# A decoder layer's w_down stage: the fourth weight sum and three operand sets split ahead of time, two weight chunks split early, and the last norms on VectorE

## The chip, the cores and the metric

The kernel runs on one core of a Trainium2 chip. The metric is device microseconds of one execution; a result is the median over several runs.

## What is computed

One post-norm decoder layer on x of 512 tokens by 1024 features, all float32:

```
p = x @ w_in                      -> u_A, v_A, q, k, v, gate_A, gate_B
y_A = GELU(u_A) * (tril(W_s) @ LN(GELU(v_A)) + b)      per chunk of 128 tokens
y_B = causal block attention over q, k, v              8 heads of 64, rotary
x = LN(alpha*x + (sig(gate_A)*(y_A @ w_a) + sig(gate_B)*(y_B @ w_b)) @ w_out)
[a | g] = causal depthwise conv3(x @ w_up)             w_up: 1024 x 5632
x = LN(alpha*x + (GELU(a)*g) @ w_down)                 w_down: 2816 x 1024
```

## The kernel before

Every float32 product is made of three fast matmuls. A tile is split into a high part, rounded by a ScalarE copy (L91), and a low part, the rest, by a VectorE subtraction (L92); `mm3` (L169) multiplies high by high, high by low and low by high. So each weight chunk (128 x 1024, half a megabyte) has to be loaded, split on two engines, and only then is multiplied. `issue` (L134) loads chunks into four raw tiles; `split_to` (L149) splits them in order, into a ring of three `wh`/`wl` pairs or, for chunks in `resident` (L115), into units of the pool `big`. After the split of chunk i it issues the load of chunk i + 4, which waits until its raw tile has been split. `chunk(i)` (L165) splits up to chunk i + 2 and hands over chunk i. The instructions of an engine run in the order in which the code issues them, and loads and stores stand in the queue of the engine that issues them, here SP.

The last two stages matter here. **w_up** (L645 to L675) takes 22 iterations n of two chunks, 48 matmuls of 128x128 by 512 columns per iteration. After the first chunk of iteration n comes `conv_ffn_tail(n - 1)` (L587): two ScalarE Identity instructions, four VectorE taps (L595), a GELU (L597), a product; for odd n - 1 also three sums and the split of the result into `fu[p]`, the left operands of w_down (p = 0 to 10). Its tiles, `cv` and `sa`, come from the pool `t4` of four buffers. **w_down** is computed with a Strassen-like scheme of seven products: it needs four plain blocks of the weights (B11, B12, B21, B22) and four sums of them (Tq, T3, T2, T4). The sums are made during w_up: `stage_load` (L628) fetches a megabyte of the four blocks for one p, `stage_add` (L632) makes four sums on VectorE, and `stage_store` (L639) writes them to `sums` in DRAM, from where they are loaded later as ordinary chunks. The stages stand at iterations 2, 3, 5, 7, ... 21.

`FIRST` (L699) is the first pass over six groups g of p (two p each, the last one) with B11, Tq, T3 and T2, 264 matmuls. Meanwhile `second_operands` (L685) makes from `fz` and `fu` the operands `fv[p]` of the second pass: two 256-column sums, two splits. `SECOND` (L743) covers groups 0 to 2 of B21, T4 and B22, then `rest` (L757) covers groups 3 to 5, one output tile of 128 tokens after the other: T4 for tokens 0 and 1, then B21 and B22 for tokens 2 and 3. `after_first` (L730) combines the first pass's results into the residual `x01b`/`x23b`. `finish` (L766) is a LayerNorm of one token tile, `norm` (L525), and its store; with `quick` false the second half of the norm is a ScalarE scaling (L539) and a GpSimd addition (L540), with `quick` true one VectorE instruction per half (L537). The last token tile's norm is written out at L791 to L803.

The pool `big` has 18 units of 8 KB per partition; a tile that finds none free waits for the last reader of an older one, a store among them.

Of the kernel before, what the change touches and what calls it, by code (L numbers as in the profile page):

```python
# [18 lines left out]
P = 128  # L19
# [34 lines left out]
TAIL = 3  # L54
FIRST = [(w, g) for g in range(len(GROUPS))
         for w in (("B11", "Tq", "T3", "T2") if g < len(GROUPS) - 1 else ("T2", "B11", "T3", "Tq"))]
SECOND = [(w, g) for g in range(TAIL) for w in ("B21", "T4", "B22")]
LAST = [(w, g) for w in ("T4", "B21", "B22") for g in range(TAIL, len(GROUPS))]
DOWN = FIRST + SECOND + LAST
C_SECOND = C_DOWN + len(FIRST)  # L60
C_LAST = C_SECOND + len(SECOND)
N_CHUNKS = C_DOWN + len(DOWN)
PLAIN = {"B11": 0, "B12": 1, "B22": 2, "B21": 3}
SUMS = {"Tq": 0, "T3": 1, "T2": 2, "T4": 3}
# [3 lines left out]
def decoder_layer(ctx: ExitStack, tc: tile.TileContext, wts, wd, xT, x, rope, wsp, par, sgu_gb, ln_gb, out):  # L68
# [18 lines left out]
    def f32(ap):  # L87
        return ap.bitcast(F32)
# [26 lines left out]
    resident = set(range(C_OUT + 4, C_OUT + 8)) | {C_UP + 3} | set(range(C_LAST, N_CHUNKS))  # L115
# [7 lines left out]
    sums = dram.tile([4, P, NQ * 512], F32, name="sums")  # L123
# [461 lines left out]
    fu, fz, held = {}, [], {}  # L585

    def conv_ffn_tail(n, ps):  # L587
        p, second = n // 2, n % 2
        ac = t4.tile([P, 2, 512], F32, tag="t4", name=f"cv{n}")
        fs = [s * NP + p + second * NQ for s in range(2)]  # L590
        for s, f in enumerate(fs):
            nc.scalar.activation(ac[:, s], ps[s], AF.Identity, bias=cb[:, f:f + 1], scale=cw[:, 2, f:f + 1])  # L592
        for s, f in enumerate(fs):
            for tap, sh in ((1, 1), (0, 2)):
                nc.vector.scalar_tensor_tensor(ac[:, s, sh:], ps[s][:, :S - sh], cw[:, tap, f:f + 1], ac[:, s, sh:],  # L595
                                               op0=ALU.mult, op1=ALU.add)
        nc.scalar.activation(ac[:, 0], ac[:, 0], AF.Gelu)  # L597
        if not second:

            held[p] = t4.tile([P, 4, 256], F32, tag="t4", name=f"sa{p}")  # L600
            nc.vector.tensor_mul(held[p][:, 2:4].rearrange("p a b -> p (a b)"), ac[:, 0], ac[:, 1])
            return
        if p % 4 == 0:
            fz.append(unit([P, 4, 2, 256], F32, f"fz{p // 4}"))
        z, sa = fz[p // 4][:, p % 4], held.pop(p)
        nc.vector.tensor_mul(z.rearrange("p a b -> p (a b)"), ac[:, 0], ac[:, 1])
        nc.vector.tensor_sub(sa[:, 0], z[:, 0], sa[:, 2])
        nc.vector.tensor_add(sa[:, 1], sa[:, 3], sa[:, 0])
        nc.vector.tensor_sub(sa[:, 2], sa[:, 3], sa[:, 2])
        fu[p] = unit([P, 2, 4, 256], F32R, f"fu{p}")  # L610
        split(fu[p][:, 0], fu[p][:, 1], sa)
# [13 lines left out]
    stage_at = {n: p for p, n in enumerate([2] + list(range(3, NP, 2)))}  # L625
# [12 lines left out]

    def stage_store(p):  # L639
        nc.sync.dma_start(sums[:, :, cols(p)].rearrange("a p c -> p a c"), stage.pop(p))  # L640
# [16 lines left out]
    for n in range(2, NP):  # L657
        ps = up_banks(n)
        for s in range(2):
            up_part(ps[s], *chunk(C_UP + 2 * n + s), 0, S)  # L660
            if s == 0:
                if n - 1 in stage_at:
                    stage_store(stage_at[n - 1])
                if n == 3:
                    for i in range(2):
                        nc.sync.dma_start(x1s[i], xres[i].rearrange("p a d -> p (a d)"))
                if n + 1 in stage_at:
                    stage_load(stage_at[n + 1])
                conv_ffn_tail(n - 1, prev)
                if n in stage_at:  # L670
                    stage_add(stage_at[n])
        prev = ps
    stage_store(NQ - 1)
    split_to(C_DOWN + 2)
    conv_ffn_tail(NP - 1, prev)  # L675


    lnp = unit([P, 2, D], F32, "lnp2")
    xres = unit([P, 2, D], F32, "x01b"), unit([P, 2, D], F32, "x23b")
# [3 lines left out]
    fv = {}  # L683
# [14 lines left out]

    for n, (w, g) in enumerate(FIRST):  # L699
        hl = chunk(C_DOWN + n)  # L700
        p0, np_ = GROUPS[g]
        for kk in range(np_):
            for i in range(2):
                prod(acc[w][i], hl, kk, fu[p0 + kk], left[w], i, p0 + kk == 0, p0 + kk == NQ - 1)
        if n == 2:
            for i in range(2):
                nc.sync.dma_start(xres[i].rearrange("p a d -> p (a d)"), x1s[i])
        if n == 6:
            nc.sync.dma_start(lnp.rearrange("p a d -> p (a d)"), ln_gb[1].partition_broadcast(P))
        if g > 0 and n % 4 in (1, 3) and g < len(GROUPS) - 1:  # L710
            second_operands(p0 - 2 + n % 4 // 2)
# [31 lines left out]
    for n, (w, g) in enumerate(SECOND):  # L743
        hl = chunk(C_SECOND + n)
# [5 lines left out]
        if n in (1, 3):  # L750
            after_first(n // 2)
        if n in (4, 6, 8):
            second_operands(NQ - 3 + (4, 6, 8).index(n))
# [3 lines left out]
    def rest(w, ps, i, start, lo=0, hi=512):  # L757
        for g in range(TAIL, len(GROUPS)):
            if (w, g) not in res:
                res[w, g] = chunk(C_LAST + LAST.index((w, g)))  # L760
# [5 lines left out]
    def finish(t):  # L766
        norm(t, sts[t], 1, False)
        nc.sync.dma_start(out[t * P:(t + 1) * P, :], xt(t))
# [108 lines left out]
```

## Time and profile before

| | us |
|---|---|
| median of 3 runs | 711.59 (711.11 to 713.39) |
| the profiled execution | 711.34 |
| its span, first to last instruction | 709.6 |
| TensorE busy | 689.1 (97%) |
| weight loads on TensorE | 568.0 (80%) |
| VectorE busy | 475.6 (67%) |
| ScalarE busy | 313.0 (44%) |
| GpSimd busy | 48.0 (7%) |

The profiled execution is 0.25 us under the median, and 1.74 us of it lie outside the span. Busy shares are means over stages with different limits; the rows further down show single stretches. PE is TensorE, DVE VectorE, ACT ScalarE, POOL GpSimd, SP the queue that issues most DMAs. A row of a timeline gives start, duration, engine, line, instruction, output, inputs and shape; in brackets stands the idle time before it and what ended it. Matmuls overlap: one of 512 columns lasts 0.39 us, and the next can begin 0.23 us after it.

### The profile page before, as it was taken

The numbers are of one execution on the slowest core, as the hardware profiler recorded it, in microseconds if no ns is written. First come the engines' busy times: TensorE is split into PE (matmuls) and PEld (weight loads), VectorE is DVE, ScalarE is ACT, GpSimd is POOL, SyncE is SP. The second block draws the span as 40 slices with busy tenths as digits, with TensorE's granted clock in tenths as the row PEclk, the third lists the DMA queues.
The fourth block names the chain that finished last, engine by engine and source line by source line (L and its number), as shares of the span: only waits on it lengthen the run. The fifth ranks groups of instructions, "written<-read, shape, count | busy, mean of one in ns | idle before, by whom it ended". The sixth has DMA issues, their size and how long they took to land.

```text
span 709.6 us, 8593 instructions
## 1 busy us (share of the span) xinstructions
PE 689.1 (97%) x3293; PEld 568.0 (80%) x3293; DVE 475.6 (67%) x721; ACT 313.0 (44%) x466; POOL 48.0 (7%) x44
## 2 busy tenths in 40 slices
PE   8999999999999999999999999999999989999875
PEld 7887888888888888888988888888888867887744
DVE  6576755454455267656588778777787695778985
ACT  5184552545445454513253444434434343556430
POOL 0213000000001000043100000000000000000042
PEclk9999999999999999999999999999999998999977
DMA  9513131222124422450159556654557548756531
GB/s 345 194 60 119 60 119 65 83 63 88 60 62 171 154 90 94 142 179 1 38 201 333 193 201 221 216 197 149 179 208 236 179 148 296 242 149 203 175 136 61
DMA packets 34841, 108.41 MB, mean 153 GB/s; under 512 B 2928, under 2 KB 3056, under 8 KB 33776
## 3 DMA queue, kind: packets, MB, share of 16 engines
q1 hardware_dynamic: 33936, 103.93, 43.1%
q0 software_dynamic: 432, 3.15, 1.1%
q10 hardware_dynamic: 432, 0.79, 0.3%
q8 instruction: 26, 0.43, 0.3%
q14 instruction: 15, 0.12, 0.1%
HBM read 92.12 MB, written 15.73 MB: 152 GB/s over the span
## 4 chain that ended last, share of the span: by engine, by line
PE 84%; DVE 8%; ACT 2%; issue 2%; DMA 2%; POOL 1%; DVEq 0%; SPq 0%; ACTq 0%; POOLq 0%
PE up L175 10%; PE up L176 10%; PE up L177 10%; PE g L175 5%; PE g L176 4%; PE g L177 4%; PE c L172 3%; PE c L173 3%; PE c L171 3%; DVE wl L92 2%; PE Y L364 2%; PE o L173 2%; PE o L171 2%; PE o L172 2%; PE tp L349 1%
## 5 line engine op out<-in xcount | busy, mean ns | idle before, releaser
L92 DVE TENSOR_TENSOR wl<-raw,wh 128x1024 fp32r<-128x1024 f32 (+1 forms) x120 | 144.0, 1206 | 135.6 <-ACT wh L91 135.2
L91 ACT ACTIVATE wh<-raw 128x1024 fp32r<-128x1024 f32 (+1 forms) x123 | 127.6, 1042 | 136.9 <-PE up L176 67.0
L175 PE MATMUL up<-x1T,wh 128*128 128x512 f32 (+1 forms) x368 | 139.3, 378 | 0.0
L177 PE MATMUL up<-x1T,wl 128*128 128x512 f32 (+1 forms) x368 | 138.1, 375 | 0.0
L176 PE MATMUL up<-x1T,wh 128*128 128x512 f32 (+1 forms) x368 | 138.1, 375 | 0.0
L176 PEld LDWEIGHTS up<-x1T,wh 128*128 128x128 f32 x368 | 69.3, 188 | 12.6
L177 PEld LDWEIGHTS up<-x1T,wl 128*128 128x128 f32 x368 | 69.2, 188 | 12.5
L175 PEld LDWEIGHTS up<-x1T,wh 128*128 128x128 f32 x368 | 69.2, 188 | 12.4
L595 DVE SCALAR_TENSOR_TENSOR cv<-up,prm,cv 128x511 f32<-128x511 f32 x88 | 63.8, 746 | 1.5
L175 PE MATMUL g<-xT,wh 128*128 128x512 f32 x128 | 52.1, 407 | 0.0
L176 PE MATMUL g<-xT,wh 128*128 128x512 f32 x128 | 50.1, 392 | 0.0
L177 PE MATMUL g<-xT,wl 128*128 128x512 f32 x128 | 50.0, 390 | 0.0
L171 PE MATMUL c<-wh,fu 128*128 128x512 f32 x88 | 35.3, 401 | 2.2 <-ACT wh L91 2.2
L172 PE MATMUL c<-wl,fu 128*128 128x512 f32 x88 | 35.6, 405 | 0.9 <-DVE wl L92 0.9
L173 PE MATMUL c<-wh,fu 128*128 128x512 f32 x88 | 35.3, 401 | 0.0
L592 ACT ACTIVATE cv<-up,prm 128x512 f32<-128x512 f32 x44 | 31.5, 764 | 3.2 <-PE up L177 3.2
L330 ACT ACTIVATE p<-s,nm 128x128 f32<-128x128 f32 (+3 forms) x32 | 16.9, 527 | 33.4 <-DVE nm L329 32.2
L530 POOL TENSOR_TENSOR rs<-rs,mhalf 128x1 f32<-128x1 f32 x7 | 6.8, 973 | 360.8 <-DVE rs L529 360.8
L175 PEld LDWEIGHTS g<-xT,wh 128*128 128x128 f32 x128 | 24.0, 188 | 7.1 <-issue 2.7
L177 PEld LDWEIGHTS g<-xT,wl 128*128 128x128 f32 x128 | 24.0, 188 | 5.4
L597 ACT ACTIVATE cv<-cv 128x512 f32<-128x512 f32 x22 | 13.9, 633 | 32.5 <-DVE cv L595 32.4
L176 PEld LDWEIGHTS g<-xT,wh 128*128 128x128 f32 x128 | 24.1, 188 | 4.1
(226 smaller groups left out, 1287.7 us busy)
## 6 DMA issues: line engine op xcount, KB each, us to landing
raw<-wts SPq DMA_DIRECT2D x95, 512.0 KB, 3.3
st<-wd SPq DMA_DIRECT2D x11, 1024.0 KB, 8.5
sums<-st SPq DMA_DIRECT2D x11, 1024.0 KB, 6.5
raw<-sums SPq DMA_DIRECT2D x20, 512.0 KB, 4.3
raw<-wd SPq DMA_DIRECT2D x15, 512.0 KB, 4.4
x<-x POOLq DMA_DIRECT2D x2, 1024.0 KB, 6.3
x1s<-x SPq DMA_DIRECT2D x2, 1024.0 KB, 10.9
xr<-xT SPq DMA_DIRECT2D x3, 512.0 KB, 7.4
```

The costliest lines, as they stand in the source:

```text
L91: nc.scalar.activation(hi, src, AF.Copy)
L92: sub.tensor_sub(lo, src, f32(hi))
L171: nc.tensor.matmul(ps, ah, wh, start=start, stop=False)
L172: nc.tensor.matmul(ps, ah, wl, start=False, stop=False)
L173: nc.tensor.matmul(ps, al, wh, start=False, stop=stop)
L175: nc.tensor.matmul(ps, wh, ah, start=start, stop=False)
L176: nc.tensor.matmul(ps, wh, al, start=False, stop=False)
L177: nc.tensor.matmul(ps, wl, ah, start=False, stop=stop)
L330: nc.scalar.activation(pr[:, s, :N], sc[s][:, :N], AF.Exp, bias=nm[:, s:s + 1], accum_out=sm[:, s:s + 1])
L364: nc.tensor.matmul(Y[hp][s * 64:s * 64 + 64, t * P:(t + 1) * P], v[:, k, (2 * hp + s) * 64:(2 * hp + s) * 64 + 64], tr[:, s, k * P:(k + 1) ...
L592: nc.scalar.activation(ac[:, s], ps[s], AF.Identity, bias=cb[:, f:f + 1], scale=cw[:, 2, f:f + 1])
L595: nc.vector.scalar_tensor_tensor(ac[:, s, sh:], ps[s][:, :S - sh], cw[:, tap, f:f + 1], ac[:, s, sh:], op0=ALU.mult, op1=ALU.add)
```

## The change

The fourth sum T4 is no longer stored as a sum and split in the second pass: `stage_split` splits it in w_up, one iteration after its stage, into a `th` tile of the pool `t4`, and `stage_store`, a further iteration later, writes three sums to `sums` and the split pair to `sum4`. The second pass loads pairs (`load_t4`) straight into units. For p = 8, 9, 10 the operands `fv` are made in the conv tail, stored to `fvs` and loaded back (`load_fv`); the other eight `second_operands` begin one group earlier. The stages now stand at iterations 2, 3, 4, 5, 7, ... 19. The last combination, p = 10, becomes `combine_last`, called in the second step of the first pass. B21 and B22 of group 0 are split in the first pass, into units. `ready` says how many of the last six chunks are split at each step of SECOND, and `after_first` moves from steps 1 and 3 to steps 0 and 1. `finish` calls `norm` with `quick` true. The reloads of x and of the norm's weights move to later steps.

```diff
@@ -52,16 +52,19 @@
 TAIL = 3
+NZ = 8
 FIRST = [(w, g) for g in range(len(GROUPS))
          for w in (("B11", "Tq", "T3", "T2") if g < len(GROUPS) - 1 else ("T2", "B11", "T3", "Tq"))]
-SECOND = [(w, g) for g in range(TAIL) for w in ("B21", "T4", "B22")]
-LAST = [(w, g) for w in ("T4", "B21", "B22") for g in range(TAIL, len(GROUPS))]
-DOWN = FIRST + SECOND + LAST
-C_SECOND = C_DOWN + len(FIRST)
-C_LAST = C_SECOND + len(SECOND)
+EARLY = {12: ("B21", 0), 16: ("B22", 0)}
+LAST = [(w, g) for w in ("B21", "B22") for g in range(TAIL, len(GROUPS))]
+DOWN = []
+for _n, _key in enumerate(FIRST):
+    DOWN += [EARLY[_n], _key] if _n in EARLY else [_key]
+DOWN += [(w, g) for g in range(1, TAIL) for w in ("B21", "B22")] + LAST
+AT = {key: C_DOWN + i for i, key in enumerate(DOWN)}
 N_CHUNKS = C_DOWN + len(DOWN)
 PLAIN = {"B11": 0, "B12": 1, "B22": 2, "B21": 3}
-SUMS = {"Tq": 0, "T3": 1, "T2": 2, "T4": 3}
+SUMS = {"Tq": 0, "T3": 1, "T2": 2}
@@ -112,7 +115,7 @@
     state = {"dma": 0, "split": 0}
-    resident = set(range(C_OUT + 4, C_OUT + 8)) | {C_UP + 3} | set(range(C_LAST, N_CHUNKS))
+    resident = set(range(C_OUT + 4, C_OUT + 8)) | {C_UP + 3} | {AT[key] for key in LAST + list(EARLY.values())}
     with_chunk = {
@@ -120,7 +123,9 @@
-    sums = dram.tile([4, P, NQ * 512], F32, name="sums")
+    sums = dram.tile([3, P, NQ * 512], F32, name="sums")
+    sum4 = dram.tile([2, P, NQ * 512], F32, name="sum4")
+    fvs = dram.tile([NQ - NZ, P, 6 * 256], F32, name="fvs")
     x1s = dram.tile([2, P, 2 * D], F32, name="x1s")
@@ -582,7 +587,7 @@
-    fu, fz, held = {}, [], {}
+    fu, fz, fv, held = {}, [], {}, {}
@@ -600,15 +605,32 @@
             return
-        if p % 4 == 0:
-            fz.append(unit([P, 4, 2, 256], F32, f"fz{p // 4}"))
-        z, sa = fz[p // 4][:, p % 4], held.pop(p)
-        nc.vector.tensor_mul(z.rearrange("p a b -> p (a b)"), ac[:, 0], ac[:, 1])
-        nc.vector.tensor_sub(sa[:, 0], z[:, 0], sa[:, 2])
-        nc.vector.tensor_add(sa[:, 1], sa[:, 3], sa[:, 0])
-        nc.vector.tensor_sub(sa[:, 2], sa[:, 3], sa[:, 2])
-        fu[p] = unit([P, 2, 4, 256], F32R, f"fu{p}")
-        split(fu[p][:, 0], fu[p][:, 1], sa)
+        if p < NZ:
+            if p % 4 == 0:
+                fz.append(unit([P, 4, 2, 256], F32, f"fz{p // 4}"))
+            z = fz[p // 4][:, p % 4]
+        else:
+            z = ac[:, 1].rearrange("p (a b) -> p a b", a=2)
+
+        def combine():
+            sa = held.pop(p)
+            nc.vector.tensor_mul(z.rearrange("p a b -> p (a b)"), ac[:, 0], ac[:, 1])
+            nc.vector.tensor_sub(sa[:, 0], z[:, 0], sa[:, 2])
+            nc.vector.tensor_add(sa[:, 1], sa[:, 3], sa[:, 0])
+            nc.vector.tensor_sub(sa[:, 2], sa[:, 3], sa[:, 2])
+            fu[p] = unit([P, 2, 4, 256], F32R, f"fu{p}")
+            split(fu[p][:, 0], fu[p][:, 1], sa)
+            if p >= NZ:
+                s4 = ac[:, 0, 0:256]
+                nc.vector.tensor_sub(s4, sa[:, 1], z[:, 1])
+                v2 = unit([P, 2, 3, 256], F32R, f"fvp{p}")
+                split(v2[:, 0, 0:2], v2[:, 1, 0:2], z)
+                split(v2[:, 0, 2], v2[:, 1, 2], s4)
+                nc.sync.dma_start(fvs[p - NZ], f32(v2.rearrange("p a b c -> p (a b c)")))
+
+        if p == NQ - 1:
+            return combine
+        combine()
@@ -622,7 +644,8 @@
     stage = {}
-    stage_at = {n: p for p, n in enumerate([2] + list(range(3, NP, 2)))}
+    stage_at = {n: p for p, n in enumerate([2, 4] + list(range(3, 20, 2)))}
+    stage_at = dict(zip(sorted(stage_at), range(NQ)))
     cols = lambda p: slice(p * 512, (p + 1) * 512)
@@ -636,8 +659,15 @@
+    def stage_split(p):
+        th = t4.tile([P, 2, 512], F32R, tag="t4", name=f"th{p}")
+        split(th[:, 0], th[:, 1], stage[p][:, 3])
+        stage[p] = stage[p], th
+
     def stage_store(p):
-        nc.sync.dma_start(sums[:, :, cols(p)].rearrange("a p c -> p a c"), stage.pop(p))
+        s, th = stage.pop(p)
+        nc.sync.dma_start(sums[:, :, cols(p)].rearrange("a p c -> p a c"), s[:, 0:3])
+        nc.sync.dma_start(sum4[:, :, cols(p)].rearrange("a p c -> p a c"), f32(th))
@@ -659,28 +689,26 @@
             if s == 0:
-                if n - 1 in stage_at:
-                    stage_store(stage_at[n - 1])
+                if n - 2 in stage_at:
+                    stage_store(stage_at[n - 2])
                 if n == 3:
...
                 conv_ffn_tail(n - 1, prev)
+                if n - 1 in stage_at:
+                    stage_split(stage_at[n - 1])
                 if n in stage_at:
...
         prev = ps
-    stage_store(NQ - 1)
-    split_to(C_DOWN + 2)
-    conv_ffn_tail(NP - 1, prev)
-
-
-    lnp = unit([P, 2, D], F32, "lnp2")
-    xres = unit([P, 2, D], F32, "x01b"), unit([P, 2, D], F32, "x23b")
+    split_to(C_DOWN + 3)
+    combine_last = conv_ffn_tail(NP - 1, prev)
+
+
     acc = {"B11": banks_of("c1", (0, 1)), "Tq": banks_of("c5", (2, 3)), "T3": banks_of("c7", (4, 5)),
...
     left = {"Tq": 0, "T2": 1, "T3": 2, "B11": 3}
-    fv = {}
@@ -696,19 +724,46 @@
+    ring_order = [key for key in FIRST + [(w, g) for g in range(TAIL) for w in ("B21", "B22")]
+                  if AT[key] not in resident]
+
+    def take(key):
+
+        split_to(AT[key] + 1)
+        n = ring_order.index(key)
+        for nxt in ring_order[n + 1:n + 3]:
+            split_to(AT[nxt] + 1)
+        return whl.pop(AT[key])
+
+    t4w = {}
+
+    def load_t4(g):
+        p0, np_ = GROUPS[g]
+        t4w[g] = unit([P, 2, CH], F32R, f"t4w{g}")
+        nc.sync.dma_start(f32(t4w[g][:, :, :np_ * 512]), sum4[:, :, p0 * 512:(p0 + np_) * 512].rearrange("a p c -> p a c"))
+
+    def load_fv(p):
+        fv[p] = unit([P, 2, 3, 256], F32R, f"fv{p}")
+        nc.sync.dma_start(f32(fv[p].rearrange("p a b c -> p (a b c)")), fvs[p - NZ])
+
     for n, (w, g) in enumerate(FIRST):
-        hl = chunk(C_DOWN + n)
+        hl = take((w, g))
+        if n == 1:
+            combine_last()
         p0, np_ = GROUPS[g]
...
                 prod(acc[w][i], hl, kk, fu[p0 + kk], left[w], i, p0 + kk == 0, p0 + kk == NQ - 1)
-        if n == 2:
-            for i in range(2):
-                nc.sync.dma_start(xres[i].rearrange("p a d -> p (a d)"), x1s[i])
-        if n == 6:
-            nc.sync.dma_start(lnp.rearrange("p a d -> p (a d)"), ln_gb[1].partition_broadcast(P))
-        if g > 0 and n % 4 in (1, 3) and g < len(GROUPS) - 1:
-            second_operands(p0 - 2 + n % 4 // 2)
+        if n % 2 and 3 <= n < 3 + 2 * NZ:
+            second_operands((n - 3) // 2)
+        if n == 15:
+            load_t4(0)
+            xres = [None, unit([P, 2, D], F32, "x23b")]
+            nc.sync.dma_start(xres[1].rearrange("p a d -> p (a d)"), x1s[1])
+        if n == 19:
+            xres[0] = unit([P, 2, D], F32, "x01b")
+            nc.sync.dma_start(xres[0].rearrange("p a d -> p (a d)"), x1s[0])
+            load_t4(1)
@@ -740,31 +795,49 @@
     right = {"T4": 0, "B21": 1, "B22": 2}
-    for n, (w, g) in enumerate(SECOND):
-        hl = chunk(C_SECOND + n)
+    ready = {0: 0, 1: 0, 2: 0, 3: 0, 4: 1, 5: 3, 6: 4, 7: 6, 8: 6}
+    for n, (w, g) in enumerate((w, g) for g in range(TAIL) for w in ("B21", "T4", "B22")):
+        if w == "T4":
+            hl = t4w[g]
+            hl = hl[:, 0], hl[:, 1]
+        elif g == 0:
+            hl = whl.pop(AT[w, g])
+        else:
+            hl = take((w, g))
+        if ready[n]:
+            split_to(AT[LAST[ready[n] - 1]] + 1)
         p0, np_ = GROUPS[g]
...
                      w == "B22" and i == 1 and p0 + kk == 2 * TAIL - 1)
-        if n in (1, 3):
-            after_first(n // 2)
-        if n in (4, 6, 8):
-            second_operands(NQ - 3 + (4, 6, 8).index(n))
+        if n in (0, 1):
+            after_first(n)
+        if n == 2:
+            load_t4(2)
+            load_fv(NZ)
+            load_fv(NZ + 1)
+        if n == 4:
+            load_fv(NZ + 2)
+        if n == 5:
+            for i in range(TAIL, len(GROUPS)):
+                load_t4(i)
+            lnp = unit([P, 2, D], F32, "lnp2")
+            nc.sync.dma_start(lnp.rearrange("p a d -> p (a d)"), ln_gb[1].partition_broadcast(P))
     nc.vector.tensor_sub(xt(3)[:, cB], xt(3)[:, cB], onto["B22"][1])
...
             if (w, g) not in res:
-                res[w, g] = chunk(C_LAST + LAST.index((w, g)))
+                res[w, g] = (t4w[g][:, 0], t4w[g][:, 1]) if w == "T4" else whl.pop(AT[w, g])
             p0, np_ = GROUPS[g]
...
     def finish(t):
-        norm(t, sts[t], 1, False)
+        norm(t, sts[t], 1, True)
         nc.sync.dma_start(out[t * P:(t + 1) * P, :], xt(t))
```

## Rows read from the trace of the kernel before

**Rows 1.** Windows: us, busy of each engine (instructions), granted clock, DMA share, GB/s.

```profile
378.00:389.00 11.00, 11.00 (x50) 9.13 (x49) 9.41 (x14) 3.67 (x5) 0.00 (x0) 1.00 1.02 409
...
576.90:592.30 15.40, 12.24 (x41) 9.31 (x41) 10.15 (x13) 6.31 (x7) 0.00 (x0) 0.78 0.63 197
...
592.30:643.70 51.40, 51.14 (x226) 41.98 (x224) 36.23 (x53) 26.80 (x39) 0.00 (x0) 1.00 0.71 233
...
643.70:681.40 37.70, 35.26 (x150) 27.76 (x150) 35.98 (x56) 17.84 (x25) 1.55 (x2) 1.00 0.56 181
...
681.40:695.00 13.60, 8.51 (x21) 5.71 (x20) 8.83 (x12) 4.27 (x6) 5.79 (x5) 0.62 0.19 77
```

**Rows 2.** Timeline of TensorE at the start of the first pass.

```profile
576.94 0.39 PE L171 MATMUL c<-wh,fu 128*128 128x512 f32 x1
...
582.15 0.39 PE L173 MATMUL c<-wh,fu 128*128 128x512 f32 x1
...
584.75 0.50 PE L171 MATMUL c<-wh,fu 128*128 128x512 f32 x1 [2.21 <-ACT wh L91]
...
586.20 0.80 PE L172 MATMUL c<-wl,fu 128*128 128x512 f32 x1 [0.95 <-DVE wl L92]
...
592.23 0.39 PE L171 MATMUL c<-wh,fu 128*128 128x512 f32 x1
```

**Rows 3.** Timeline of ScalarE and VectorE in w_up and at its end.

```profile
390.60 1.22 DVE L92 TENSOR_TENSOR wl<-raw,wh 128x1024 fp32r<-128x1024 f32 x1
...
565.54 1.06 ACT L91 ACTIVATE fu<-sa 128x1024 fp32r<-128x1024 f32 x1 [5.89 <-DMA sums<-st]
...
577.64 2.97 DVE L595 SCALAR_TENSOR_TENSOR cv<-up,prm,cv 128x511 f32<-128x511 f32 x4
...
583.78 1.22 DVE L92 TENSOR_TENSOR fu<-sa,fu 128x1024 fp32r<-128x1024 f32 x1 [1.12 <-ACT fu L91]
...
584.92 3.49 DVE L92 TENSOR_TENSOR wl<-raw,wh 128x1024 fp32r<-128x1024 f32 x3
```

**Rows 4.** Timeline of TensorE in the second pass.

```profile
643.71 0.50 PE L171 MATMUL c<-wh,fv 128*128 128x512 f32 x1 [0.28 <-ACT keptT L719]
...
681.26 0.39 PE L173 MATMUL c<-res,fv 128*128 128x512 f32 x1
...
686.17 0.80 PE L171 MATMUL c<-res,fv 128*128 128x512 f32 x1 [4.53 <-ACT res L91]
...
694.71 0.39 PE L173 MATMUL c<-res,fv 128*128 128x512 f32 x1
...
701.85 0.28 PE L173 MATMUL c<-res,fv 128*128 128x256 f32 x1
```

**Rows 5.** Groups by line and form, 352 us to the end: count, busy, mean.

```profile
L92 DVE TENSOR_TENSOR wl<-raw,wh 128x1024 fp32r<-128x1024 f32 x69 | 83.6, 1222 | 50.9 <-ACT wh L91 50.7
...
L92 DVE TENSOR_TENSOR fv<-fz,fv 128x512 fp32r<-128x512 f32 x11 | 7.5, 685 | 0.0
```

**Rows 6.** Timeline of VectorE in the second pass and the tail.

```profile
645.66 1.28 DVE L520 SCALAR_TENSOR_TENSOR x23b<-x23b,c 128x512 f32<-128x512 f32 x2
...
649.35 0.69 DVE L520 SCALAR_TENSOR_TENSOR x23b<-x23b,keptT 128x512 f32<-128x512 f32 x1
...
653.57 0.75 DVE L523 BATCH_NORM_STATS2 st<-x01b 128x6 f32<-128x256 f32 x2
...
676.92 0.68 DVE L773 TENSOR_TENSOR x01b<-x01b,c 128x512 f32<-128x512 f32 x1
...
678.79 1.40 DVE L533 SCALAR_TENSOR_TENSOR x01b<-x01b,mv,lnp 128x512 f32<-128x512 f32 x2
...
702.16 0.42 DVE L785 TENSOR_TENSOR x23b<-x23b,c 128x256 f32<-128x256 f32 x1 [0.91 <-PE c L173]
```

**Rows 7.** DMA issues: size of each, median us from issue to landing.

```profile
x23b<-x1s SPq DMA_DIRECT2D x1, 1024.0 KB, 10.7
...
raw<-sums SPq DMA_DIRECT2D x4, 256.0 KB, 2.7
```

## The prediction

> **What bounds the kernel now.** First the windows: TensorE has no idle time where w_up runs at the granted clock 1.00, and it loses time in two places only [rows 1]. Between 576.9 and 592.3 us it is busy for 12.24 of 15.40 us at a mean clock of 0.78; between 681.4 and 695.0 us for 8.51 of 13.60 us at 0.62. From 643.7 to 681.4 us VectorE is busy for 35.98 of 37.70 us: the second pass is bound by VectorE, which splits weights, prepares operands and combines there, while the first pass (36.23 of 51.40 us) is not.
>
> Then the timeline of TensorE, for the price of each place. Its pace is (582.15 - 576.94)/23 = 0.2265 us per 512-column matmul [rows 2]. At the start of the first pass the 25th matmul was due at 582.38; full pace is back at 592.23, 15 matmuls later, which need 3.40 us: 6.45 us are lost. The third chunk's `wl` came 3.59 us late (second matmul due 582.61, begun 586.20), and then the matmuls ran at half pace, the lower level of the clock (1.2 GHz), for another 2.86. What was late is read from the other engines [rows 3]: ScalarE stood 5.89 us behind a `fu` tile whose memory a stage store still held, and VectorE came to the third chunk's `wl` only after the last conv tail, at 584.92.
>
> In the second pass, 183 matmuls of 512 columns and 30 of 256 (0.12 each) need 45.1 us from 643.71; the last ends at 701.97, so 13.2 us are lost [rows 4], most of them behind 681.26, where a weight split sat on ScalarE behind the norms and the clock then fell.
>
> **The change part by part.**
>
> *Work moved into w_up.* Each of 11 stages gains one 512-column split, 0.69 us of VectorE by the `fv` form [rows 5], and three operand pairs gain a sum and two splits, 0.42 + 0.69 + 0.42 = 1.53 us each: 7.5 + 4.6 = 12.1 us of VectorE. Cover: chunks are split two ahead, and an iteration like that of 378 to 389 us leaves VectorE free for 1.6 of 11 us [rows 1]. The tightest spot is iteration 5, as stages now sit at 2, 3, 4 and 5: its second chunk's `wl` ended at 391.8 [rows 3] and was due 16.5 iterations of 48 matmuls before 576.94, at 397.5. Ahead of it come two splits and the four sums of a new stage, 2 x 0.69 + 2.77 = 4.2 us: it ends at 396.0, 1.5 us early, and the next iteration has no combination. I take nothing; if the lead is less than this, up to 2 us of wait, once.
>
> *DMAs in w_up.* A stage writes 1.25 MB in two stores in place of 1 MB, three more stores write operands. The heaviest iteration, the third (x1s out, 2 MB), ran at 409 GB/s [rows 1]; it now loads a stage, but stores none. Taken as nothing: two splits and four raw tiles lie between a load and its use.
>
> *End of w_up.* The last stage moves from iteration 21 to 19, and one `fz` unit goes, so the 5.89 us wait goes. What is late next: `split_to(C_DOWN + 3)` puts the third chunk ahead of the tail. It waits for the ring buffer of the last w_up chunk, free at about 577.1; `wh` 1.06, `wl` until 579.4, in time for 582.4. The four taps (2.97 [rows 3]) end at 582.4, the fourth chunk's `wl` at 584.0, due at 585.3. But `combine_last` is issued ahead of the fifth chunk's split on ScalarE and VectorE. From the last tap (580.61) to the end of the `fu` split (585.00) this work took 4.4 us before [rows 3]; now it ends at 588.4, the pair for p = 10 follows, ScalarE reaches the fifth `wh` at about 589.1, and `wl` ends at 591.4. It is due as second matmul at 588.05: 3.35 us late against 3.59 before. So the wait moves by two chunks and shrinks by 0.25 us. Its clock cost lies between nothing and the 2.86 us of before. The nearest row is that of before, where waits of 2.21 and 0.95 us took the clock down [rows 2]; the new ones, about 2.1 and 1.1, are their like, so I take 2.86: gain 0.25 us.
>
> The Trainium skill ("TensorE: Matmul & The Clock Gate", Part 1) says that the array's recent activity sets its clock and that the moment of judgement isn't tied to the kernel's start. By this rule nearly the same idle time may fall either way; the row alone says it falls.
>
> *First pass.* Two chunk splits (1.22 each), `combine_last` and earlier `second_operands` go onto a VectorE that had 15 of 51 us free [rows 1]: nothing. The loads of t4w0, x23b, x01b and t4w1 (4 MB) stand among raw loads on SP's queue; four raw tiles cover them.
>
> *Second pass.* Out of VectorE go 5.5 chunk splits of T4 (6.7 us), those of B21 and B22 of group 0 (2.4) and three `second_operands` (3 x 1.95, the pair's 1.53 and another sum), 15 us where it was 95% busy. So all 13.2 us of TensorE's loss could go. Two things come back.
>
> First, SP. All loads stand in one queue, and a raw load waits until its buffer has been split. VectorE is free of the copies at 646.94, spends 2 x 4.97 us (649.35 to 654.32, [rows 6]) on `after_first`, now back to back, and splits B21(2), B22(2), B21(3), B21(4) until 658.1, 659.3, 660.5 and 661.7. The raw load of the last chunk waits for that, and the loads of t4w3, t4w4, t4w5 and `lnp2` stand behind it, at 662 to 663.5. Ahead of them on the DMA engines are 2.25 MB of raw tiles and fv10. At 409 GB/s (2.56 us per MB) with some 2 us until landing (256 KB took 2.7, of which 0.64 is transfer [rows 7]) they land at about 669.4, 671.9, 673.2 and 675.8. TensorE wants t4w3 at 643.71 + 108 x 0.2265 = 668.2: a wait of 1.2; six matmuls later t4w4: 1.1; t4w5 and `lnp2` are in time. Cost 2.3 us. Bounds: nothing, if they land as alone; 4 us, if they land as late as the 10.7 us of x23b [rows 7].
>
> Second, the norms. `finish` leaves ScalarE and GpSimd, and VectorE takes 1.40 us more for each of three. A norm with its sum and stats is then 1.87 (676.92 to 678.79) + 2 x 1.35 = 4.6 us [rows 6]. Tokens end 3.4 us apart on TensorE, so VectorE runs full from the first T4 end on: 4.6 + 4.6 + 1.4 + 4.6 + 1.4 + 0.9 = 17.5 us to the last L785, against 17.1 us of TensorE's. Cost 0.4 us, bounds 0 and 1. From L785 at 702.16 to the end nothing changes.
>
> **Sum.** Second pass -13.2 + 2.3 + 0.4 = -10.5; start of the first pass -0.25. The span of 709.6 us becomes 698.8; 711.34 - 709.6 = 1.74 lie around it, and the profiled run stands 0.25 under the median of 711.59. So 711.59 - 10.75 = **700.8 us**.
>
> **Rivals.**
>
> *A, the clock holds* at the fifth chunk: 2.86 less, 697.9. For it: the new idle time is a little shorter. Against it: the waits before [rows 2].
>
> *B, the T4 loads come in time*: 2.3 less, 698.5; with A 695.6. For it: the windows show the queue far from full in the second pass (0.56 [rows 1]). Against it: it is empty because SP waits.
>
> *C, the clock also falls at the T4 waits*, or the loads come later: 2.9 more, 703.7; with the wait of 2 in iteration 5, 705.7. Against it: the smaller waits before 681 us left the clock at 1.00 [rows 1].
>
> *D, slower*: the new `th` tiles share four buffers with the conv tails and are held until both stores have landed. If a store took longer than about 20 us (the next `th` in the same buffer), ScalarE would stand there with the weight splits behind it. One such wait is 5.89 us [rows 3]; less a lead of some 3 us, 11 stages cost 32 us: about 733. Against it: one megabyte took 10.7 us behind 2.5 others [rows 7].
>
> *E, nothing moves*: the second pass gives its waits back as waits for loads: 711. Against it: 15 us leave the engine that bounds it.
>
> **Chances.** Forecast 0.42, A 0.23, B with or without A 0.14, C 0.15, D 0.04, E 0.02. All but D and E are faster by over 0.3% (2.1 us, about what a measurement of this kernel can tell from no change): faster 0.94, same 0.02, slower 0.04. The range goes from B with A, 695.5, to C with its wait, 705.5.
>
> **What would show it.** Right: TensorE's wait for `wl` at the start of the first pass stands at the fifth chunk, with 3 to 3.5 us; no wait for `res` on ScalarE; TensorE waiting about 2 us for a DMA into t4w3 or t4w4; VectorE without a gap from the first `finish` to the end; no PE wait in w_up. Wrong: a PE wait inside w_up, a wait of ScalarE for a store, or the second pass with the clock below 1.00 before its last matmuls.

## The result and the profile after

The changed kernel takes 699.66 us (699.61 to 702.1, 4 runs) against 711.46 (711.11 to 713.39, 4 runs): a ratio of 0.9837 [0.981, 0.9865]. The forecast was 700.8 us, from 695.5 to 705.5. The profiled execution took 702.1 us, 2.4 more than the median, with a span of 700.1; it stands against the 709.6 of before.

First the waits of TensorE in the changed kernel (engine, tile, line, what it waited for: us in total, times, longest):

```profile
PE c L176 <- DMA t4w<-sum: 2.3, 1, 2.3
PE c L176 <- ACT wh L94: 1.7, 1, 1.7
PE c L176 <- ACT keptT L774: 1.6, 1, 1.6
...
PE c L177 <- DVE wl L95: 0.8, 1, 0.8
```

The two left out belong to the start of the kernel, and a last one of 0.2 us lies ahead of w_up. All others are in three places: the start of the first pass, its end, and T4 in the second pass. The windows, with columns as in [rows 1]:

```profile
378.00:389.00 11.00, 11.00 (x50) 9.12 (x49) 10.29 (x15) 3.36 (x5) 0.00 (x0) 1.00 1.02 398
577.20:595.40 18.20, 15.76 (x61) 12.32 (x61) 14.51 (x21) 9.75 (x13) 0.00 (x0) 0.91 0.50 173
595.40:643.50 48.10, 46.50 (x206) 38.13 (x205) 34.80 (x50) 26.67 (x37) 0.00 (x0) 1.00 0.78 262
643.50:667.90 24.40, 24.40 (x108) 20.17 (x108) 20.19 (x28) 9.13 (x12) 0.00 (x0) 1.00 0.85 321
667.90:674.00 6.10, 3.83 (x11) 2.62 (x10) 1.29 (x2) 0.63 (x1) 0.00 (x0) 0.72 1.04 418
674.00:692.00 18.00, 18.00 (x93) 15.39 (x92) 15.90 (x33) 0.00 (x0) 2.77 (x3) 1.00 0.26 103
```

In w_up (378 to 389) VectorE went from 9.41 to 10.29 us of 11 and TensorE has no gap, as before [rows 1]. In the second pass up to T4 VectorE is busy for 20.19 of 24.40 us, where it was 35.98 of 37.70 [rows 1], and TensorE runs there without a gap for 24.4 us. The timeline of TensorE gives the sum:

```profile
577.24 0.39 PE L176 MATMUL c<-wh,fu 128*128 128x512 f32 x1
...
589.97 0.50 PE L176 MATMUL c<-wh,fu 128*128 128x512 f32 x1 [1.69 <-ACT wh L94]
591.23 0.50 PE L177 MATMUL c<-wl,fu 128*128 128x512 f32 x1 [0.76 <-DVE wl L95]
...
591.80 0.62 PE L176 MATMUL c<-wh,fu 128*128 128x512 f32 x1
...
595.44 0.39 PE L176 MATMUL c<-wh,fu 128*128 128x512 f32 x1
...
643.47 0.50 PE L176 MATMUL c<-res,fv 128*128 128x512 f32 x1 [1.60 <-ACT keptT L774]
...
667.86 0.39 PE L178 MATMUL c<-wh,fv 128*128 128x512 f32 x1
670.52 0.80 PE L176 MATMUL c<-t4w,fv 128*128 128x512 f32 x1 [2.27 <-DMA t4w<-sum]
...
673.25 0.61 PE L176 MATMUL c<-t4w,fv 128*128 128x512 f32 x1
...
673.93 0.39 PE L178 MATMUL c<-t4w,fv 128*128 128x512 f32 x1
...
692.59 0.28 PE L178 MATMUL c<-res,fv 128*128 128x256 f32 x1
```

From the second pass's first matmul to the last it took 58.14 us before (643.71 to 701.85 [rows 4]) and takes 49.12 now: -9.02. The first pass went from 66.77 to 66.23: at its start 4.60 us are lost where 6.45 were, at its end 1.3 more than before. It starts 0.30 later, and the end behind the last matmul is 0.24 shorter. Together -9.5 us, the difference of the spans.

What was late is in the timelines of the other two engines (against [rows 3]); first VectorE at the start of the first pass:

```profile
579.45 2.97 DVE L600 SCALAR_TENSOR_TENSOR cv<-up,prm,cv 128x511 f32<-128x511 f32 x4
...
583.83 0.69 DVE L617 TENSOR_TENSOR cv<-cv 128x512 f32<-128x512 f32 x1
...
586.90 1.23 DVE L95 TENSOR_TENSOR fu<-sa,fu 128x1024 fp32r<-128x1024 f32 x1 [1.13 <-ACT fu L94]
...
589.95 2.36 DVE L95 TENSOR_TENSOR wl<-raw,wh 128x1024 fp32r<-128x1024 f32 x2 [0.52 <-ACT wh L94]
```

The combination (583.83 to 589.4) stands between the taps and the fifth chunk's `wl`; the wait of 5.89 us for a store [rows 3] is gone. And ScalarE at the first pass's end:

```profile
641.88 1.06 ACT L94 ACTIVATE wh<-raw 128x1024 fp32r<-128x1024 f32 x1 [1.62 <-PE c L178]
642.84 2.04 ACT L774 ACTIVATE keptT<-c 128x512 f32<-128x512 f32 x4
```

The copies `keptT`, for which TensorE waits until 643.47, stand behind the split of B22(1) (B22 of group 1). For the idle time ahead of that split the profile names a matmul, but the last one that read this ring buffer's older chunk began at 640.12 and lasts 0.39 us. The chunk's load was issued at 635.18 us and took 6.6 us to land, so the split waited for its raw tile. In e8 below, the trace names the load itself:

```profile
639.33 1.06 ACT L94 ACTIVATE wh<-raw 128x1024 fp32r<-128x1024 f32 x1 [2.05 <-DMA raw<-wd]
```

### The profile page after: what moved, and what is told of

It is laid out like the page before. It is cut to its first block, busy times and chain, and to the rows that moved or that the text cites. A ratio compares the mean times of both kernels' runs of the same rounds, so it can differ in the third digit from the quotient of the medians.

```text
span 700.1 us, 8629 instructions
## 1 busy us (share of the span) xinstructions
PE 684.1 (98%) x3293; PEld 566.2 (81%) x3293; DVE 476.6 (68%) x729; ACT 309.4 (44%) x465; POOL 40.0 (6%) x38
## 4 chain that ended last, share of the span: by engine, by line
PE 87%; DVE 8%; DMA 2%; ACT 1%; issue 1%; POOL 0%; DVEq 0%; SPq 0%; ACTq 0%
PE up L181 11%; PE up L180 11%; PE up L182 11%; PE g L180 5%; PE g L181 4%; PE g L182 4%; PE c L176 3%; PE c L177 3%; PE c L178 3%; PE Y L369 2%; PE o L177 2%; PE o L178 2%; PE o L176 2%; DMA t4w<-sum 1%; PE tp L354 1%; DVE st L528 1%
## 5 line engine op out<-in xcount | busy, mean ns | idle before, releaser
L95 DVE TENSOR_TENSOR wl<-raw,wh 128x1024 fp32r<-128x1024 f32 (+1 forms) x115 | 137.8, 1206 | 123.5 <-ACT wh L94 123.1
L94 ACT ACTIVATE wh<-raw 128x1024 fp32r<-128x1024 f32 (+1 forms) x118 | 122.4, 1040 | 128.1 <-PE up L181 61.5
```

The source lines that it names most:

```text
L94: nc.scalar.activation(hi, src, AF.Copy)
L95: sub.tensor_sub(lo, src, f32(hi))
```

## The experiments

All of them were timed in turn with the kernel before, whose median on the chips used was 709.6 to 710.7 us; the ratio is to that, and the range in brackets is its 95% interval.

**The changed kernel once more (e1).**

> The changed kernel as it is, timed beside the others. Its profiled run took 702.1 us, three runs without a profile 699.6 to 699.7. If the clock falls in some executions and holds in others at the two waits of TensorE (fifth chunk, t4w3; together 1.7 + 2.2 us at half clock in the profiled run), single times should lie at 699.6 or some 2 us above, nothing between; if the profile itself costs 2.4 us, only the profiled run lies at 702.

701.25 us (698.92 to 702.72, 5 runs), ratio 0.9864 [0.9847, 0.988]. Neither alternative held: the times are 698.92, 700.47, 701.25, 701.5 and 702.72 us, and the profiled one is the second fastest. Their mean granted clock goes with them in the main: 0.996 at 698.92 and 700.47, 0.990 at 702.72. The window from the first pass's start to 600 us shows one place of it, in four kernels that are the same up to there. The changed kernel's window:

```profile
577.20:600.00 22.80, 20.36 (x81) 16.08 (x81) 17.79 (x26) 12.50 (x17) 0.00 (x0) 0.93 0.54 177
```

The same in this run (e1):

```profile
577.40:600.00 22.60, 20.16 (x88) 16.15 (x87) 18.40 (x27) 12.89 (x18) 0.00 (x0) 1.00 0.55 184
```

In e3, below:

```profile
577.80:600.00 22.20, 19.76 (x73) 15.51 (x72) 16.78 (x25) 11.34 (x15) 0.00 (x0) 0.85 0.52 169
```

In e4, below:

```profile
577.00:600.00 23.00, 20.56 (x89) 16.44 (x89) 18.76 (x27) 13.20 (x18) 0.00 (x0) 1.00 0.57 188
```

All four have the same two waits, 1.7 and 0.76 us, in the same place. The clock held in two and fell to the half level in two, for different lengths. Against the pace of 0.2265 us per matmul, 4.6, 3.0, 5.9 and 3.1 us are lost by 600 us; the chunk is 2.9 us late in all four, so the clock's share is 1.7, about nothing, 3.0 and about nothing.

**The last combination later (e2).** The combination p = 10 goes from step 1 of the first pass to step 2, behind the fifth chunk's split; its operand pair to step 18.

```diff
-        if n == 1:
+        if n == 2:
             combine_last()
+        if n == 18:
+            pair_last()
```

> The last combination is called at step 2 of the first pass, after the split of the fifth chunk was issued, and the operand pair of p = 10 at step 18. Theory 1 (the order on ScalarE and VectorE makes the wait at the fifth chunk): the waits of 1.69 and 0.76 us vanish or shrink below 0.5, the clock stays up there, and the time falls by the 2.9 us of the wait, by up to 4.6 with its clock: 695 to 697 us. Rival (the fifth chunk's weights land late): the wait stays, 699.7.

697.81 us (697.58 to 698.62, 5 runs), 0.982 [0.9807, 0.9833], 3.4 us under e1 on the same chip, and 0.8 above the forecast. TensorE's only waits from the start of the first pass on:

```profile
PE c L176 <- ACT keptT L781: 2.1, 1, 2.1
PE c L176 <- DMA t4w<-sum: 1.3, 2, 0.9
```

So the wait at the fifth chunk came from the combination ahead of its split. Part of the gain came back at once: the first pass ends earlier, and `keptT` waits 2.1 us instead of 1.6.

**The T4 loads earlier (e3).** The loads of t4w3 to t4w5 go from step 5 of the second pass to step 2, ahead of the raw loads that wait for buffers.

```diff
         if n == 2:
             load_t4(2)
             load_fv(NZ)
             load_fv(NZ + 1)
+            for i in range(TAIL, len(GROUPS)):
+                load_t4(i)
```

> The loads of t4w3 to t4w5 are issued at step 2 of the second pass, ahead of the raw loads that wait for VectorE. Theory 1 (SP's queue holds them back): they land before 662, TensorE's wait of 2.27 us at t4w3 goes with its half clock, together 4.0 us in the profiled run; 696 to 697.5 us. Rival (VectorE's chain of norms, or the norm's weights behind the same queue, sets the end): the wait goes, the norms start later against TensorE, and under 1 us is won: 698.7 to 699.7.

699.07 us (696.71 to 700.2, 5 runs), 0.9826 [0.9807, 0.9845], 2.2 us under e1, which was timed beside it. No wait for `t4w` is left: that wait came from the place of the loads in SP's queue. The time itself misses theory 1 and lies in the rival's range, as both were reckoned from 699.7; in this profile 5.9 us were lost at the first pass's start, as shown above.

**Both (e8).** The edits of e2 and e3 together:

> The changed kernel with both edits: the last combination at steps 2 and 18, the T4 loads at step 2 of the second pass. Theory 1 (two separate causes, their gains add): no wait above 0.5 us in the first pass and none at t4w3; 694 to 696 us, and single times within 1 us, since nothing is left that lets the clock fall. Rival (the last chain on VectorE takes back what the T4 loads give): 697 to 698, as with the combination alone.

695.03 us (694.75 to 697.13, 4 runs), 0.9793 [0.9773, 0.9812]. The time is as forecast, and the gains nearly add up (some 5 us under e1 by the ratios, 3.4 and 2.2 alone). The rest of the forecast missed: single times scatter by 2.4 us, and one wait is left, at the first pass's end and longer than before:

```profile
PE c L176 <- ACT keptT L781: 2.4, 1, 2.4
```

**The norms back on ScalarE and GpSimd (e4)** in the changed kernel (`quick` false in `finish`).

> The changed kernel with the three norms on ScalarE and GpSimd again. Theory 1 (what the second pass gained comes from the splits and operands moved out of it; the norms on VectorE cost 0.4 us at the end): 698.9 to 699.8 us, no wait of TensorE behind a split on ScalarE. Rival (the 4.53 us wait for a split on ScalarE went because the norms left ScalarE): that wait comes back with its clock, 704 to 709 us.

700.32 us (699.33 to 701.29, 4 runs), 0.9854 [0.984, 0.9868]: the same as e1 within its scatter, 0.5 us above the forecast, and no wait behind a split on ScalarE. The last matmul begins at 690.05 and the last VectorE instruction at 692.97, 2.92 us later, exactly as in the changed kernel (692.59 and 695.51). The norms' place was worth nothing in it that can be measured.

**The norms alone (e5)**, on the kernel before (`quick` true).

> The kernel before with only the norms of finish on VectorE. Theory 1 (VectorE holds the second pass back; the wait named for a ScalarE split would only become a wait for the VectorE half of the same split): 709.5 to 712 us, TensorE's wait of 4.5 us stays within 1 us in sum. Rival (the norms on ScalarE and GpSimd cause the wait): it goes with its clock, 9.4 us, to about 701.5.

708.97 us (707.27 to 711.17, 12 runs), 0.9984 [0.9971, 0.9998], half a microsecond under the forecast. The large wait stays and changes its name: where 4.53 us went to ScalarE's half of a split [rows 4], they now go to VectorE's half of it:

```profile
688.83 0.79 PE L172 MATMUL c<-res,fv 128*128 128x512 f32 x1 [4.81 <-DVE res L92]
```

**The stages alone (e6)**, on the kernel before, so that the last one no longer ends the loop.

```diff
-    stage_at = {n: p for p, n in enumerate([2] + list(range(3, NP, 2)))}
+    stage_at = {n: p for p, n in enumerate([2, 3, 4] + list(range(5, 20, 2)))}
```

> The kernel before with the stages at iterations 2, 3, 4, 5, 7 to 19, nothing else. Theory 1 (the 5.89 us wait for a store puts the last tail 1 to 2 us behind, the order of tail and split does the rest): that wait goes, TensorE's wait at the third chunk shrinks by 1 to 2 us and stays above 1, 707 to 710 us. Rival A (the store's wait is the whole cause): no wait there, 704. Rival B (it is hidden): 710.7.

708.78 us (706.98 to 709.55, 12 runs), 0.9975 [0.9963, 0.9988]. The wait for `wh` halves, from 2.21 [rows 2] to 1.14; the one for `wl` stays at 0.95:

```profile
584.07 0.50 PE L171 MATMUL c<-wh,fu 128*128 128x512 f32 x1 [1.14 <-ACT wh L91]
585.52 0.50 PE L172 MATMUL c<-wl,fu 128*128 128x512 f32 x1 [0.95 <-DVE wl L92]
```

**No early chunks (e7).** The changed kernel with `EARLY = {}`: B21 and B22 of group 0 are split in their order, at the end of the first pass, instead of in its middle.

> The changed kernel with B21 and B22 of group 0 split in order again, in the second pass. Theory 1 (VectorE's queue sets when the raw tiles come free and so when the T4 loads are issued): VectorE has 2.4 us more before the last raw load, t4w3 lands that much later, and TensorE's wait there grows from 2 to 4 or 4.5 us; 701.5 to 704 us. Rival (VectorE has room, 5.8 us idle ahead of the first norm): as the changed kernel, 699 to 701.

708.71 us (707.89 to 711.13, 12 runs), 0.9985 [0.9974, 0.9997]. Nearly all of the change's gain is gone, far more than the two splits' 2.4 us: both forecasts missed by 4 us and more. SP's queue shows why:

```profile
636.16 21.32 SPq L149 DMA_DIRECT2D raw<-wd  x6
657.57 0.39 SPq L743 DMA_DIRECT2D t4w<-sum  x1
...
664.11 4.00 SPq L743 DMA_DIRECT2D t4w<-sum  x3
```

ScalarE waited for those loads:

```profile
661.34 1.06 ACT L94 ACTIVATE res<-raw 128x1024 fp32r<-128x1024 f32 x1 [7.71 <-DMA raw<-wd]
668.37 0.63 ACT L94 ACTIVATE res<-raw 128x512 fp32r<-128x512 f32 x1 [5.96 <-DMA raw<-wd]
```

And TensorE for its weights:

```profile
657.17 0.50 PE L177 MATMUL c<-wl,fv 128*128 128x512 f32 x1 [2.65 <-DVE wl L95]
...
676.07 0.80 PE L176 MATMUL c<-t4w,fv 128*128 128x512 f32 x1 [6.31 <-DMA t4w<-sum]
```

SP stood for 21 us in six raw loads. Each waits until its raw tile has been split; the fifth was issued at 646.24, and the last at 657.15, when VectorE had come through `after_first` to the split of that tile (from 655.91 on). The loads of t4w2 and of the first two `fv` stood behind it. In the changed kernel SP had them out 13 us earlier, and came to the same stand only then:

```profile
644.60 0.43 SPq L743 DMA_DIRECT2D t4w<-sum  x1
645.08 0.93 SPq L747 DMA_DIRECT2D fv<-fvs  x2
657.66 2.60 SPq L149 DMA_DIRECT2D raw<-wd  x3
```

The two chunks split early are what puts these loads ahead of that stand. One thing more differs in e7: the two chunks go through the ring of three instead of units, and ScalarE waited there for TensorE (2.63 and 1.66 us ahead of its splits at 648.90 and 651.62). What the ring costs by itself was not tried.

**The end of the first pass (e9).** Two loads of e8's kernel are moved, to see whether they delay the raw tile of B22(1), whose split stands on ScalarE ahead of the `keptT` copies:

```diff
-        if n == 19:
+        if n == 17:
             xres[0] = unit([P, 2, D], F32, "x01b")
             nc.sync.dma_start(xres[0].rearrange("p a d -> p (a d)"), x1s[0])
+        if n == 22:
             load_t4(1)
```

> e8's kernel (late combination, T4 loads early) with two loads moved in the first pass: x01b from step 19 to step 17, the second T4 pair (t4w1) from step 19 to step 22, behind the raw loads of the first second-pass chunks. Theory 1 (the keptT wait at the end of the first pass comes from the raw tile of B22(1), which shares the DMA engines with the two 1 MB loads issued with it): that raw lands about 2.5 us earlier, ScalarE splits it and reaches the keptT copies in time, the wait of 2.43 us goes to under 0.5 and the clock holds: 693 to 694 us where e8 took 695.0. Rival (the wait is set by ScalarE's order of work or by VectorE, not by the load): the wait stays above 1.5 us and the time at 695. Second rival: t4w1 is now late for its matmuls at step 4 of the second pass, and TensorE waits there for t4w instead: 695 to 697.

698.72 us (697.93 to 699.25, 4 runs), 0.9834 [0.982, 0.9847]: slower than e8. The tile was split at 639.09, 62.1 us behind the pass's first matmul (576.95); in e8 it was 61.5 (639.33 and 577.80). The tile's load was issued 53.8 us behind that matmul in both, and took 7.7 us to land in e8 and 8.3 here. Theory 1 fell: moving the loads that were issued with it brings it no earlier. The rival's wait came, but its time did not: 698.72 lies above all three forecasts. The wait for `keptT` grew to 3.31 us, and the clock fell behind it to 0.52 for six microseconds:

```profile
640.60:646.60 6.00, 5.92 (x14) 4.64 (x15) 5.83 (x10) 3.40 (x7) 0.00 (x0) 0.52 0.98 368
```

**The operands made in the first pass (e10)**, in e8's kernel: `second_operands` for all eleven p, no store of `fv` and no load.

```diff
-NZ = 8
+NZ = NQ
...
+OPS = [1, 4, 6, 7, 9, 10, 12, 13, 15, 17, 18]
...
-        if n % 2 and 3 <= n < 3 + 2 * NZ:
-            second_operands((n - 3) // 2)
+        if n in OPS:
+            second_operands(OPS.index(n))
```

> e8's kernel with the three operand sets fv8 to fv10 made in the first pass by second_operands, as the other eight, and not in w_up, so that they are neither stored to DRAM nor loaded back (4.5 MB of transfers less; three operand sets of VectorE work more in the first pass, 3 x 2 us, where VectorE has some 13 us free). Theory 1 (the gain of the change needs these sets out of the second pass, not in w_up and DRAM): no new wait of TensorE for VectorE in the first pass, and the keptT wait shrinks because fewer loads share the engines: 693.5 to 695. Rival (they have to be made in w_up, the first pass has no room): TensorE waits 1 to 3 us for wl somewhere in the first pass or at the second pass's first fv, 696 to 699.

696.48 us (696.29 to 698.02, 4 runs), 0.9808 [0.9794, 0.9821], an interval that overlaps e8's. The wait for `keptT` is 1.11 us, and two waits come at the start of the pass (0.37 and 0.95), of which this operand work, ahead of a split, is the likely cause; a third comes later in it (0.69). The time is in the rival's range. Against e8, neither way of making the operands is measurably faster.

**Loads apart and operands together (e11).** The edits of e9 and e10 on e8's kernel.

> Both edits of e9 and e10 on e8's kernel. If both theories 1 hold: no wait of TensorE over 0.5 us from the start of the first pass to the end, 692.5 to 694. If the keptT wait comes from ScalarE's or VectorE's order: 695 to 697.

698.45 us (697.17 to 701.98, 5 runs), 0.9851 [0.9829, 0.9872]. Above both forecasts: waits of 0.2 to 1.2 us in six places, that for `keptT` 1.24, and no gain.

**The copies first (e12).** The split of B22(1) behind the `kept` copies, in e8's kernel:

```diff
-        for nxt in ring_order[n + 1:n + 3]:
+        for nxt in ring_order[n + 1:n + (2 if key == FIRST[-1] else 3)]:
...
                 residual(2 + i, acc["B11"][i], 0, 512)
+    split_to(AT["B22", 1] + 1)
```

> e8's kernel with the split of B22(1) issued behind the copies of the first pass's results (keptT2, keptT3, keptTq) instead of ahead of them; nothing else moves, and that chunk is first used five steps later, at about 652 us. e9 moved two of the loads and the wait stayed, so the theory is now: the copies stand on ScalarE behind a weight split whose raw tile lands at 639 to 642 us whatever is moved by two steps, because the DMA engines are full from about 622 us on. Then this edit takes the wait for keptT out (2.43 us in e8) and what it cost in clock: 692 to 693 us, with no wait of TensorE over 0.5 us from the start of the first pass to the end. Rival: the same lateness comes back one step on, as a wait at the start of T4 for VectorE to free the banks of B11, or as a wait for wl of B21(1) or B22(1): 694.5 to 696.

695.38 us (694.86 to 695.57, 5 runs), 0.9797 [0.978, 0.9814]. The wait is gone, and the first pass takes 60.24 us (577.67 to 637.91) where it took 63.12 in e8's profile. The median stays. (e8's profiled execution, whose clock fell behind the wait, took 697.13 us; its other three took 694.75 to 695.04.) From the first pass on TensorE waits once:

```profile
666.59 0.47 PE L176 MATMUL c<-t4w,fv 128*128 128x512 f32 x1 [1.32 <-DMA fv<-fvs]
...
684.47 0.28 PE L178 MATMUL c<-res,fv 128*128 128x256 f32 x1
```

VectorE's timeline shows the rest:

```profile
662.75 0.69 DVE L95 TENSOR_TENSOR res<-raw,res 128x512 fp32r<-128x512 f32 x1 [6.86 <-ACT res L94]
...
669.09 0.68 DVE L854 TENSOR_TENSOR x01b<-x01b,c 128x512 f32<-128x512 f32 x1
...
686.19 0.40 DVE L866 TENSOR_TENSOR x23b<-x23b,c 128x256 f32<-128x256 f32 x1
```

The last addition on VectorE begins 1.72 us behind the last matmul; in the changed kernel it was 0.32 (692.91 and 692.59). From 669.09 on VectorE runs without a gap, and what kept it from starting earlier are the last weight splits: the last of them began at 667.22 on ScalarE, after 1.51 us of waiting for its raw load, and ended at 668.57 on VectorE. So the rival held, in another place than it named: the lateness went past TensorE's next steps into VectorE's tail. Whether the norms on ScalarE would pay in this kernel, where VectorE ends last, was not tried. e8 and e12 are equal within their intervals, and both beat the changed kernel by about 5 us (0.9793 and 0.9797 against 0.9864).

## Why the prediction was right, and where not

*w_up at no cost*: right. From 352 us to the first pass VectorE is busy for 186.0 us where it was 175.9 (12.1 more were reckoned, with the operands of p = 10, which come behind that stretch). This and the stores show in no wait of TensorE there, and ScalarE waited for no store, so D fell.

*Start of the first pass*: the place was right, and so was its cause (e2). The waits are 1.69 and 0.76 us, not 2.1 and 1.1, and the chunk came 2.88 us late (591.23 where 588.35 was due), not 3.35. The term that was mis-sized is the clock's, taken as 2.86 us: 1.72 here (4.60 lost in all), 3.0 in e3, and about nothing in e1 and e4. So the forecast's fall and rival A's holding clock each came in two of four profiles. The Trainium skill ("TensorE: Matmul & The Clock Gate", Part 1) says that the moment of judgement isn't tied to the kernel's start, from which the prediction took that nearly the same idle time may fall either way; the traces agree, with 0.93, 1.00, 0.85 and 1.00 behind the same two waits.

*First-pass loads at nothing*: this step failed. The wait at the pass's end went from 0.28 us [rows 4] to 1.60 in both profiles of the changed kernel (0.27 and 0.49 in e3 and e4, whose first pass is the same). Four raw tiles cover a late load only if ScalarE has nothing else to do behind it; here the `keptT` copies stood behind the split of a chunk that is needed five steps later. e12 shows that order as the cause of the wait. Why the tile is late is not settled: its load took 6.6 us to land, 7.7 in e8 and 8.3 in e9, where the median of the 15 of its size and source in the changed kernel is 4.7, and the DMA engines were near full (a share of 0.98 in e8 and 1.01 in e9 from 622 to 636 us). e9 shows only that moving two of the loads by two or three steps does not bring it sooner.

*Second pass*: the 13.2 us went, as computed. (2.44 of them lay between 643.7 and 681.4, where TensorE was busy for 35.26 of 37.70 us [rows 1]: a third place of loss, where the prediction names two.) The T4 wait is where it was put (SP's queue, e3); t4w3 was used at 670.52 instead of 669.4. But it is one wait of 2.27 us at t4w3, not 1.2 there and 1.1 at t4w4, and the sum of the waits came out at the 2.3 by chance. The three loads were issued within two microseconds:

```profile
661.48 1.92 SPq L743 DMA_DIRECT2D t4w<-sum  x3
```

Their times from issue to landing, in the order of issue:

```profile
t4w<-sum SPq DMA_DIRECT2D x1, 1024.0 KB, 9.0
...
t4w<-sum SPq DMA_DIRECT2D x1, 1024.0 KB, 10.8
t4w<-sum SPq DMA_DIRECT2D x1, 512.0 KB, 11.5
```

With issues at 661.48, 662.27 and 662.83 us they landed at 670.5, 673.1 and 674.3: one behind the other, as reckoned, and each 1.1 to 1.2 us later than forecast (669.4, 671.9, 673.2). There is no wait at t4w4 because the clock fell behind the first wait (0.72 in the window above): the six matmuls of t4w3 took from 670.52 to 673.25, and by then t4w4 had landed. In e4, where the first of these matmuls ran at full clock, the second wait is there, with 0.42 us. The slow matmuls cost 1.6 us. At full clock, by an estimate from these landings, some 1.1 of it would have been the wait at t4w4. So both halves of rival C came, loads that are late and a clock that falls, to which I had given 0.15. One sign of being wrong came with it: the clock below 1.00 in the second pass at 667.9 to 674.0 us, where its last matmul begins at 692.59. The signs of being right came too, but for the size of the lateness at the fifth chunk.

*Norms*: VectorE ran from the first `finish` to the end without a gap, as said, at 4.52 us per token (4.6 computed). Cost: nothing that can be measured in the changed kernel (e4) where 0.4 was taken.

*The sum*: the profiled execution lies 9.5 us under that of before where 10.75 were forecast: 1.1 more clock saved at the first pass's start and 0.4 on the norms and 0.5 less lateness, against 1.3 at `keptT`, 1.7 more at T4 (4.0 lost there, with the clock, where 2.3 were taken) and the 0.3 of a later start. Errors of 2.0 us one way and 3.3 the other nearly cancel, so it is partly luck that the sum came this close. The median gained 11.8: the three executions beside the profiled one had a mean clock of 0.996 to 0.998 where it had 0.993, which fits a clock that held in more places, but no profile shows them. In e1 the median gained 9.5, so the forecast of 10.75 lies between the two measurements. What the reasons left out is how the gain hangs together: they counted the two early chunks as 2.4 us off VectorE, and e7 shows that without them the rest of the change gains almost nothing, since SP's queue then stands. The norms alone (e5) and the stages alone (e6) are worth 1 to 2 us on the kernel before. The splits of T4 were not moved by themselves, so their share of the gain is argued from VectorE's and TensorE's rows, not shown.

## What to carry to other kernels

When loads wait for buffers in one queue, ask what stands behind the first load that waits: two chunks split in idle time of an earlier stage were worth some 8.6 us (0.9985 less 0.9864 of 710), most likely because they let the loads behind go out before the queue stood, and loads whose own buffers are free belong ahead of it. When a wait is taken out, follow the work to the next engine that has none to spare: here from TensorE's start to the copies, from them to a load and to VectorE's tail. A copy that the next stage waits for should not be issued behind a split that is needed five steps later.

## What was not expected of the hardware

The same pair of waits (1.7 and 0.76 us) left the granted clock at 1.00 in two profiles and brought it to the half level in two others, for 1.7 us of loss in one and 3.0 in the other. A wait of 2.43 us (e8's) took it down for part of the window behind it, one of 3.31 (e9) for all of it, while with no wait (e12) it stayed at 1.00. The six microseconds behind e8's wait:

```profile
640.90:646.90 6.00, 5.98 (x19) 4.76 (x20) 5.83 (x10) 3.47 (x6) 0.00 (x0) 0.72 1.03 414
```

And the same stretch of e12, without it:

```profile
637.90:643.90 6.00, 6.00 (x28) 4.97 (x27) 5.67 (x9) 2.43 (x5) 0.00 (x0) 1.00 1.02 415
```

Loads took long where the DMA engines were full: in the changed kernel, with a share of 1.00 from 661.4 to 674.0 us, a megabyte of `t4w` took 9.0 and 10.8 us from issue to landing, and 768 KB of `fv` had a median of 12.9 over the kernel, where 256 KB took 2.7 in the kernel before [rows 7]. No run shows one of these loads by itself.
